# GpSimd adds the four feature blocks of the attention output's squares before TensorE sums over features

## The chip, the cores and the metric

The kernel runs on one core of a Trainium2 chip. The metric is the device time of one execution in microseconds (us). TensorE is called PE in the profile (PEld is its weight load), VectorE DVE, ScalarE ACT, GpSimd POOL and SyncE, which issues the loads and stores, SP.

## What is computed

One layer of a diffusion backbone for 128 context tokens and 512 latent tokens, with 1024 features, all in float32. Attention (8 query heads, 2 key heads of 64 features) and a gated short convolution run side by side, each gives 512 features, each is normalised over these, and one output projection joins them. A feed-forward part follows. The piece that matters:

```python
def _rms(x, g):
    y = x * lax.rsqrt(jnp.mean(x * x, axis=-1, keepdims=True) + RMS_EPS)
    return y * g

def _mixer(h, ...):
    proj = h @ w_in                       # q, k, v and the conv's gb, gc, u
    ...
    attn = _block_attention(q_r, k_all, v_all)       # (tokens, 512)
    y_conv = gb * _short_conv(gc * u, conv_w)        # (tokens, 512)
    merged = jnp.concatenate([_rms(attn, attn_out_norm), _rms(y_conv, conv_out_norm)], axis=-1)
    return merged @ w_out, k, v
```

The change touches the sum of `attn * attn` over the 512 features of a token, which is the first half of `_rms(attn, attn_out_norm)`.

## The kernel before, in words

The 640 tokens are five tiles of 128: tiles 0 to 3 are latent, tile 4 (`CTX`) is the context. Every product of two float32 matrices is made of three matmuls on rounded halves (`mm3`, L155 to L157; the convolution's own are L710 to L712). Each tile that such a matmul reads is made by `split`: ACT writes the rounded half (L151), DVE the rest (L152).

The span has four stages. Up to about 60 us inputs are loaded, normalised and modulated. From there to about 258 us attention and convolution run interleaved. The order of PE's instructions there is written out in the string `SEQ`: `S` are the scores of one head, `T` the transposes of its probabilities, `O` their product with the values, `Q` a transpose of queries, `F1` one step of the convolution as filler, and `r` the call of `att_rms`. From 258 to about 320 us the output projection runs, token tile by token tile in two halves of columns, and then the feed-forward part, to the end.

PE follows the program's order everywhere. In attention and projection DVE, ACT, POOL and SP follow an order that a scheduler set when the kernel was built, from its own costs and from the priorities in the code (`early`). Each engine takes its instructions strictly in that order, so an instruction that waits holds back all behind it on its engine.

The softmax of one head (`att_s`): PE writes the scores into `ps` (L824); DVE takes the maximum (L830); ACT scales it (L831) and takes the exponential (L834); DVE takes the reciprocal of the sum (L836); DVE (L840, first head of a pair) or ACT (L838, second head) scales the probabilities. The next scores wait until L834 has read `ps`, of which there is one buffer. `att_t` transposes the probabilities on PE (L851) and splits them, and `att_o` multiplies them with the values (L868).

When a pair of key and value heads of one tile is done, ACT copies its result out of PSUM (L875, for the context L934), SP moves halves of it across partitions by two DMAs into `es` (L883, L884), DVE adds (L889, L890), and `of[t]` holds 256 of the tile's 512 features: features on partitions, in four blocks of 128, tokens along the free dimension. ACT squares these into `osq[t]` (L891). For tile 3 `osq[t]` lies in the buffer `oz`. `v` is 0 for the first 256 features and 1 for the second.

`att_rms(t)` sums the squares over the features: the block of squares is PE's stationary operand, a column of ones the moving one, and the four blocks are added in PSUM. DVE then scales the sum (L163, `ms`), and POOL takes the power -1/2 (L165, `rA`). It is called for the context tile long after its attention, for tiles 0, 1 and 2 one or two units after theirs, and for tile 3 inside the output projection. There `conv_rms` has made the like factors `rB` for the convolution's half (L796 on PE, L163, L165), and each projected tile is scaled with `rA` (L1117 on ACT) and `rB` (L1118 on DVE), multiplied by a gate (L1120) and added to the input (L1121). L1029 are multiply-adds on DVE for a later gate, and L248 is DVE's half of the split of the output projection's weights.

Of the kernel before, what the change touches and what calls it, by code (L numbers as in the profile page):

```python
# [12 lines left out]
ALU = mybir.AluOpType  # L13
# [78 lines left out]
def build(ctx, tc, x_prompt, x_sample, c, cache_k, cache_v, c_ctx, norm_mix, norm_ffn, w_ada, b_ada,  # L92
# [3 lines left out]
    act, dve, pool, pe, sp = nc.scalar, nc.vector, nc.gpsimd, nc.tensor, nc.sync  # L96
# [23 lines left out]
    def T(tag, shape, dt=F32, bufs=1):  # L120
        seq[0] += 1
        return pools[where.get(tag, "A")][1].tile(list(shape), dt, tag=tag, bufs=bufs, name=f"{tag}_{seq[0]}")

    def PB(shape=(P, 512), dt=F32, tag="t"):
        seq[0] += 1
        if kept.get(tag):
            w = kept[tag].pop()
            n = 1
            for y in shape[1:]:
                n *= y  # L130
            w = w[:, :n] if tag != "s" else w
            if tag != "s" and len(shape) > 2:
                names = "abc"[:len(shape) - 1]
                w = w.rearrange("p (" + " ".join(names) + ") -> p " + " ".join(names), **dict(zip(names, shape[1:])))
            return w
        return pools["psum"][1].tile(list(shape), dt, tag=tag, bufs=pbufs[tag], name=f"p{tag}_{seq[0]}")
# [13 lines left out]
    def split(hi, lo, src):  # L150
        act.activation(hi, src, AF.Copy)  # L151
        dve.tensor_tensor(lo, src, f32(hi), ALU.subtract)  # L152
# [6 lines left out]
    def rstd_of(ss, n, scale, by=1.0, tag="rs"):  # L159

        w = ss.shape[1]
        ms = T("ms", (P, w), F32, 4)
        dve.tensor_scalar(ms, ss, scale * by, EPS * by, ALU.mult, ALU.add)  # L163
        r = T(tag, (P, w), F32, {"rB": 1, "rs": 6}.get(tag, NT))
        pool.tensor_tensor(r, ms, neghalf[:, :w], ALU.pow)  # L165
        return r
# [202 lines left out]
    ones = T("ones", (P, P))  # L369
# [445 lines left out]
    oe, osq = {}, {}  # L815
# [42 lines left out]
    def att_o(u, g):  # L858
        t, v, p = u[0:3]
        kts = GRPS[g]  # L860
        if g == 0:
            u[5] = PB((P, 2, P), tag="o")
        ov = u[5].rearrange("p a q -> p (a q)")
        last = g == len(GRPS) - 1
        for i, kt in enumerate(kts):
            w = VS[:, kt + 1, v].rearrange("p a d -> p (a d)")
            for n, x in enumerate(u[4][g]):
                pe.matmul(ov, w, x[:, i].rearrange("p a q -> p (a q)"), start=(g == 0 and i == 0 and n == 0),  # L868
                          stop=(last and i == len(kts) - 1 and n == 1))
        if not last:  # L870
            return
        if p == 0:
            oe[t, v] = T2((P, 2, 2, P))
        e = oe[t, v]
        act.activation(e[:, p], u[5], AF.Copy)  # L875
        if p == 0:
            return
        att_add(t, v, e)

    def att_add(t, v, e):  # L880

        esw = T("es", (P, 2, P))
        sp.dma_start(esw[0:64], e[64:128, :, 0, :])  # L883
        sp.dma_start(esw[64:128], e[0:64, :, 1, :])  # L884
        if v == 0:
            of[t] = T("of", (P, 4, P), F32, NT)
            osq[t] = T("osq", (P, 4, P), F32, OSQ) if t != NL - 1 else T("oz", (P, 4, P))
        o = of[t][:, 2 * v:2 * v + 2]
        dve.tensor_tensor(o[0:64], e[0:64, :, 0, :], esw[0:64], ALU.add)  # L889
        dve.tensor_tensor(o[64:128], e[64:128, :, 1, :], esw[64:128], ALU.add)  # L890
        act.activation(osq[t][:, 2 * v:2 * v + 2], o, AF.Square)  # L891
        if t == CTX:
            split(mix_ctx[0][:, 2 * v:2 * v + 2], mix_ctx[1][:, 2 * v:2 * v + 2], o)

# [33 lines left out]
    def ctx_o(v):  # L928
        ov = PB((P, 2, 2, P), tag="o")
        w = VS[:, 0, v].rearrange("p a d -> p (a d)")  # L930
        for n, x in enumerate(cu[v]):
            pe.matmul(ov.rearrange("p a b q -> p (a b q)"), w, x.rearrange("p h q -> p (h q)"), start=(n == 0), stop=(n == 1))
        e = T2((P, 2, 2, P))
        act.activation(e, ov, AF.Copy)  # L934
        att_add(CTX, v, e)

    def att_rms(t):
        sps = PB((P, 1))
        for p in range(4):
            pe.matmul(sps, osq[t][:, p], ones[:, 0:1], start=(p == 0), stop=(p == 3))  # L940
        rA[t] = rstd_of(sps, 1, 1.0 / 512, tag="rA")

    def unit(t, v, p):
# [10 lines left out]
    def rms_of(t):  # L954
        if t == CTX or t >= 0:
            att_rms(t)
# [121 lines left out]
    for j in range(2):  # L1078
        cols = slice(j * 512, (j + 1) * 512)
        for n, t in enumerate(TORD):  # L1080
# [23 lines left out]
            if j == 0 and n == 1:  # L1104
                att_rms(NL - 1)
                act.activation(warm, rA[NL - 1], AF.Silu)
# [25 lines left out]
            with early(XP[j]):  # L1132
# [3 lines left out]
                else:  # L1136
                    q = T("ms", (P, 1), F32, 4)
# [223 lines left out]
```

## Time and profile before

| what | value |
|---|---|
| runs, median (lowest to highest) of 3 | 758.66 us (757.63 to 758.73) |
| profiled execution: span from first to last instruction | 755.2 us |
| PE busy | 737.5 us, 98% |
| DVE busy | 551.7 us, 73% |
| ACT busy | 378.8 us, 50% |
| POOL busy | 42.6 us, 6% |
| chain that ended last: PE, DVE, ACT | 83%, 7%, 5% |

The page tells the profiled execution's span and no other time for it. The median of the timed runs lies 3.5 us above the span (758.66 - 755.2), for what lies ahead of the first and behind the last instruction. A PE that is busy for 98% says that it rarely stands idle in sight of the profile; matmuls overlap their neighbours, and a wait of under 0.15 us is not shown as one.

A row of the timeline has the start and the duration in us, the engine, the line, the operation, what it writes and reads, and how often it follows itself; in brackets stand the engine's idle time before it and what ended that. A row of the chain has start, duration and what.

### The profile page before, as it was taken

The numbers are of one execution on the slowest core, as the hardware profiler recorded it, in microseconds if no ns is written. First come the engines' busy times: TensorE is split into PE (matmuls) and PEld (weight loads), VectorE is DVE, ScalarE is ACT, GpSimd is POOL, SyncE is SP. The second block draws the span as 40 slices with busy tenths as digits, with TensorE's granted clock in tenths as the row PEclk, the third lists the DMA queues.
The fourth block names the chain that finished last, engine by engine and source line by source line (L and its number), as shares of the span: only waits on it lengthen the run. The fifth ranks groups of instructions, "written<-read, shape, count | busy, mean of one in ns | idle before, by whom it ended". The sixth has DMA issues, their size and how long they took to land.

```text
span 755.2 us, 11953 instructions
## 1 busy us (share of the span) xinstructions
PE 737.5 (98%) x4618; PEld 665.2 (88%) x4618; DVE 551.7 (73%) x997; ACT 378.8 (50%) x745; POOL 42.6 (6%) x75
## 2 busy tenths in 40 slices
PE   7999899999999999999999999999999999999997
PEld 5678888988998887899998799998889998899986
DVE  5558877666666798779979778884678866788653
ACT  5356777667656534765552235553125541255410
POOL 2403101011000110100000000000000000000000
PEclk9999999999999999999999999999999999999999
DMA  9985133532432464031235313133113232222312
GB/s 290 294 236 163 51 104 102 165 92 91 159 107 91 133 224 138 1 112 54 81 118 157 108 58 110 58 111 112 56 56 104 67 112 78 62 86 84 112 56 83
DMA packets 101389, 84.52 MB, mean 112 GB/s; under 512 B 3502, under 2 KB 81650, under 8 KB 101332
## 3 DMA queue, kind: packets, MB, share of 16 engines
q1 hardware_dynamic: 100980, 83.39, 35.9%
q8 instruction: 36, 0.59, 0.3%
q0 software_dynamic: 352, 0.37, 0.3%
q14 instruction: 21, 0.17, 0.1%
HBM read 79.68 MB, written 2.75 MB: 109 GB/s over the span
## 4 chain that ended last, share of the span: by engine, by line
PE 83%; DVE 7%; ACT 5%; DMA 2%; issue 1%; SPq 1%; POOL 0%; ACTq 0%
PE pf L155 17%; PE pf L157 17%; PE pf L156 17%; PE pc L710 3%; PE pc L712 3%; PE pc L711 3%; PE po L868 3%; PE ps L824 2%; PE ph L155 2%; PE ph L157 2%; PE ph L156 2%; PE pc L388 2%; PE pt L851 2%; DMA wf<-in_w_in_dram 1%; PE ps L155 1%
## 5 line engine op out<-in xcount | busy, mean ns | idle before, releaser
L151 ACT ACTIVATE wh<-wf 128x512 fp32r<-128x512 f32 (+1 forms) x68 | 55.5, 816 | 81.1 <-PE pf L157 59.3
L155 PE MATMUL pf<-wh,gT 128*128 128x512 f32 (+1 forms) x225 | 86.9, 386 | 0.0
L156 PE MATMUL pf<-wl,gT 128*128 128x512 f32 (+1 forms) x225 | 86.5, 385 | 0.0
L157 PE MATMUL pf<-wh,gT 128*128 128x512 f32 (+1 forms) x225 | 86.5, 384 | 0.0
L710 PE MATMUL pc<-hH,wh 128*128 128x320 f32 x192 | 61.1, 318 | 0.0
L712 PE MATMUL pc<-hH,wl 128*128 128x320 f32 x192 | 59.3, 309 | 0.0
L711 PE MATMUL pc<-hL,wh 128*128 128x320 f32 x192 | 59.3, 309 | 0.0
L152 DVE TENSOR_TENSOR wl<-wf,wh 128x1024 fp32r<-128x1024 f32 (+1 forms) x34 | 39.4, 1160 | 25.2 <-ACT wh L151 22.1
L155 PE MATMUL pf<-T,wh 128*128 128x320 f32 x160 | 49.6, 310 | 0.5 <-ACT u L1191 0.5
L156 PEld LDWEIGHTS pf<-wl,gT 128*128 128x128 f32 x225 | 42.3, 188 | 8.6 <-issue 0.2
L155 PEld LDWEIGHTS pf<-wh,gT 128*128 128x128 f32 x225 | 42.3, 188 | 8.6 <-issue 0.2
L157 PEld LDWEIGHTS pf<-wh,gT 128*128 128x128 f32 x225 | 42.3, 188 | 8.3
L156 PE MATMUL pf<-T,wh 128*128 128x320 f32 x160 | 49.4, 309 | 0.0
L155 PE MATMUL pf<-T,wl 128*128 128x320 f32 x160 | 49.4, 309 | 0.0
L156 PE MATMUL pf<-T,wl 128*128 128x320 f32 x160 | 49.4, 309 | 0.0
L157 PE MATMUL pf<-T,wl 128*128 128x320 f32 x160 | 49.4, 309 | 0.0
L157 PE MATMUL pf<-T,wh 128*128 128x320 f32 x160 | 49.4, 309 | 0.0
L155 PE MATMUL pf<-B,wl 128*128 128x320 f32 x152 | 47.1, 310 | 0.0
L157 PE MATMUL pf<-B,wl 128*128 128x320 f32 x152 | 47.0, 309 | 0.0
L156 PE MATMUL pf<-B,wl 128*128 128x320 f32 x152 | 47.0, 309 | 0.0
L155 PE MATMUL pf<-B,wh 128*128 128x320 f32 x136 | 42.2, 310 | 1.5 <-DVE cu L1220 1.5
L151 ACT ACTIVATE wl<-wf 128x512 fp32r<-128x512 f32 x34 | 21.2, 625 | 41.6 <-PE pf L156 34.8
(306 smaller groups left out, 2058.7 us busy)
## 6 DMA issues: line engine op xcount, KB each, us to landing
wf<-in_w_gate_up_dram SPq DMA_DIRECT2D x44, 512.0 KB, 4.0
aw<-in_w_ada_dram SPq DMA_DIRECT2D x24, 512.0 KB, 4.1
wf<-in_w_down_dram SPq DMA_DIRECT2D x20, 512.0 KB, 3.3
wf<-in_w_in_dram SPq DMA_DIRECT2D x18, 512.0 KB, 5.5
af<-in_w_ada_dram SPq DMA_DIRECT2D x32, 256.0 KB, 6.4
x<-in_x_sample_dram SPq DMA_DIRECT2D x8, 512.0 KB, 6.2
wf<-in_w_out_dram SPq DMA_DIRECT2D x8, 512.0 KB, 4.4
wf<-in_w_ada_dram SPq DMA_DIRECT2D x8, 512.0 KB, 3.7
```

Source lines behind the costliest of these rows:

```text
L151: act.activation(hi, src, AF.Copy)
L152: dve.tensor_tensor(lo, src, f32(hi), ALU.subtract)
L155: pe.matmul(out, lh, rh, start=start, stop=False, skip_group_check=more)
L156: pe.matmul(out, lh, rl, start=False, stop=False, skip_group_check=more)
L157: pe.matmul(out, ll, rh, start=False, stop=stop, skip_group_check=more)
L388: pe.matmul(out[CG * g:CG * (g + 1)], cp[:, k], w, start=(k < 4), stop=(k >= KD - 4), skip_group_check=True)
L710: pe.matmul(acc, wh[:, k], hH[k][:, c0:c0 + n], start=(k == 0), stop=False)
L711: pe.matmul(acc, wh[:, k], hL[k][:, c0:c0 + n], start=False, stop=False)
L712: pe.matmul(acc, wl[:, k], hH[k][:, c0:c0 + n], start=False, stop=(k == KD - 1))
L824: pe.matmul(s2[:, g, :320], q, kk[:, v, P + g * 320:P + (g + 1) * 320], start=(i == 0), stop=(i == 1))
L851: pe.transpose(tp[:, i, h], u[3][h][:, kt * P:(kt + 1) * P], ident)
L868: pe.matmul(ov, w, x[:, i].rearrange("p a q -> p (a q)"), start=(g == 0 and i == 0 and n == 0), stop=(last and i == len(kts) - 1 and n == 1))
```

## The change

When the second half of a tile's squares has been written (`v` is 1), POOL adds features 256 to 511 to features 0 to 255, and then the second of the two remaining blocks to the first, in place. One matmul per tile then sums the 128 partitions of the first block, in place of four.

```diff
         act.activation(osq[t][:, 2 * v:2 * v + 2], o, AF.Square)
+        if v:
+            q = osq[t]
+            pool.tensor_tensor(q[:, 0:2], q[:, 0:2], q[:, 2:4], ALU.add)
+            pool.tensor_tensor(q[:, 0], q[:, 0], q[:, 1], ALU.add)
...
     def att_rms(t):
         sps = PB((P, 1))
-        for p in range(4):
-            pe.matmul(sps, osq[t][:, p], ones[:, 0:1], start=(p == 0), stop=(p == 3))
+        pe.matmul(sps, osq[t][:, 0], ones[:, 0:1], start=True, stop=True)
         rA[t] = rstd_of(sps, 1, 1.0 / 512, tag="rA")
```

The line numbers behind L891 grow by three or four: the adds are L894 and L895, the matmul of `att_rms` is L943 where it was L940. PE and ACT keep their order, but for the 15 matmuls that go.

POOL's order, first piece: the context tile. `c` is the convolution's padded buffer, `rq` the factor of a tile's queries. Before:

```order
L165 TENSOR_TENSOR rs_1078<-ms_1076,neghalf_176 128x2
L165 TENSOR_TENSOR rq_1237<-ms_1235,neghalf_176 128x8
L729 MEMSET c_291_1263 128x1 x4
L165 TENSOR_TENSOR rA_1514<-ms_1512,neghalf_176 128x1
L165 TENSOR_TENSOR rq_1573<-ms_1571,neghalf_176 128x8
```

Now:

```order
L165 TENSOR_TENSOR rs_1078<-ms_1076,neghalf_176 128x2
L165 TENSOR_TENSOR rq_1239<-ms_1237,neghalf_176 128x8
L729 MEMSET c_291_1265 128x1 x4
L894 TENSOR_TENSOR osq_1112<-osq_1112 128x256
L895 TENSOR_TENSOR osq_1112<-osq_1112 128x128
L165 TENSOR_TENSOR rA_1513<-ms_1511,neghalf_176 128x1
L165 TENSOR_TENSOR rq_1572<-ms_1570,neghalf_176 128x8
```

The two adds stand where POOL had nothing to do until `rA`.

POOL's order, second piece: tiles 2 and 3, up to the factors of the output projection. Before:

```order
L751 TENSOR_TENSOR ysum_727<-ysum_727,c_601_2718 128x512
L751 TENSOR_TENSOR ysum_727<-ysum_727,c_601_2718 128x128
L729 MEMSET c_654_2942 128x1 x4
L165 TENSOR_TENSOR rA_2855<-ms_2853,neghalf_176 128x1
L751 TENSOR_TENSOR ysum_727<-ysum_727,c_707_3221 128x512
L751 TENSOR_TENSOR ysum_727<-ysum_727,c_707_3221 128x128
L165 TENSOR_TENSOR rB_3315<-ms_3313,neghalf_176 128x5
L165 TENSOR_TENSOR rA_3397<-ms_3395,neghalf_176 128x1
```

Now:

```order
L751 TENSOR_TENSOR ysum_727<-ysum_727,c_601_2715 128x512
L751 TENSOR_TENSOR ysum_727<-ysum_727,c_601_2715 128x128
L894 TENSOR_TENSOR osq_2514<-osq_2514 128x256
L895 TENSOR_TENSOR osq_2514<-osq_2514 128x128
L729 MEMSET c_654_2938 128x1 x4
L165 TENSOR_TENSOR rA_2851<-ms_2849,neghalf_176 128x1
L751 TENSOR_TENSOR ysum_727<-ysum_727,c_707_3217 128x512
L751 TENSOR_TENSOR ysum_727<-ysum_727,c_707_3217 128x128
L894 TENSOR_TENSOR oz_3007<-oz_3007 128x256
L895 TENSOR_TENSOR oz_3007<-oz_3007 128x128
L165 TENSOR_TENSOR rB_3313<-ms_3311,neghalf_176 128x5
L165 TENSOR_TENSOR rA_3392<-ms_3390,neghalf_176 128x1
```

Tile 2's adds stand ahead of the convolution's memsets, and tile 3's adds ahead of `rB`.

DVE's order at tile 2's `att_rms`; `nsr` holds a head's softmax scalars, `ms` the scaled sum of squares. Before:

```order
L889 TENSOR_TENSOR of_2516<-t_583_2624,es_2759 64x256
L890 TENSOR_TENSOR of_2516<-t_583_2624,es_2759 64x256
L152 TENSOR_TENSOR pl_2812<-pt_2808,ph_2811 128x256
L830 TENSOR_REDUCE nsr_2820<-ps_2815 128x1
L836 RECIPROCAL nsr_2820<-nsr_2820 128x1
L163 TENSOR_SCALAR ms_2853<-pt_2848 128x1
L830 TENSOR_REDUCE nsr_2866<-ps_2861 128x1
```

Now:

```order
L889 TENSOR_TENSOR of_2513<-t_583_2621,es_2756 64x256
L890 TENSOR_TENSOR of_2513<-t_583_2621,es_2756 64x256
L152 TENSOR_TENSOR pl_2811<-pt_2807,ph_2810 128x256
L830 TENSOR_REDUCE nsr_2819<-ps_2814 128x1
L163 TENSOR_SCALAR ms_2849<-pt_2847 128x1
L836 RECIPROCAL nsr_2819<-nsr_2819 128x1
L830 TENSOR_REDUCE nsr_2862<-ps_2857 128x1
```

`ms`, which waits for the matmul on the squares, now stands ahead of the softmax's reciprocal.

## The prediction

> **What bounds the kernel now.** I read the page first, then the chain that ended last for the five matmul groups that change, then the stages around them.
>
> ```profile
> span 755.2 us, 11953 instructions
> ...
> PE 737.5 (98%) x4618; PEld 665.2 (88%) x4618; DVE 551.7 (73%) x997; ACT 378.8 (50%) x745; POOL 42.6 (6%) x75
> ...
> PE 83%; DVE 7%; ACT 5%; DMA 2%; issue 1%; SPq 1%; POOL 0%; ACTq 0%
> ```
>
> PE carries the span and POOL is nearly empty, so taking work from PE to POOL can pay. The chain shows where the removed matmuls lie (start, duration, what):
>
> ```profile
> 116.65 0.79 PE pt L940 x8
> 155.13 1.05 PE pt L940 x8
> 195.40 0.79 PE pt L940 x8
> 226.18 0.79 PE pt L940 x8
> 270.93 0.79 PE pt L940 x8
> ```
>
> In this order they are the context tile and tiles 0, 1, 2, 3. All five lie on the chain. Four matmuls show as eight passes, each of which loads 128 columns of squares to multiply them with a single column. But PE is not equally the bound everywhere. Three stretches (length, then PE, PEld, DVE, ACT, POOL busy):
>
> ```profile
> 90.00:120.00 30.00, 28.11 (x199) 24.52 (x198) 23.02 (x44) 21.55 (x46) 1.13 (x1) 1.00 0.37 115
> 180.00:210.00 30.00, 30.00 (x225) 27.81 (x225) 19.38 (x39) 20.58 (x44) 0.56 (x1) 1.00 0.35 115
> 262.00:292.00 30.00, 30.00 (x147) 25.21 (x146) 28.21 (x48) 14.08 (x27) 3.27 (x2) 1.00 0.61 208
> ```
>
> From 180 to 210 PE never stands. At 90 to 120 it waits for 1.89 us: the softmax paces it. From 262 to 292 DVE has 28.21 of 30 us, as good as full, and whatever delays DVE there comes back to PE.
>
> **What goes.** Of eight passes two stay. Six of eight in 0.79 us are 0.59 us a tile (tile 2: 226.02 to the next instruction's start is about the same), 2.96 us for five. I take 0.59 for tile 0 as well, whose 1.05 holds a wait for a PSUM buffer.
>
> What of it is kept depends on what is late next. For the context tile, tile 0 and tile 1 I found no wait behind the matmul that began ahead of it and ends within 0.6 us of its need, so each keeps 0.59: 1.77. Tile 2 is different:
>
> ```profile
> 224.01 0.42 ACT L891 ACTIVATE osq<-of 128x256 f32<-128x256 f32 x1 [0.66 <-DVE of L890]
> 224.35 0.81 DVE L830 TENSOR_REDUCE nsr<-ps 128x1 f32<-128x640 f32 x1
> ...
> 226.02 0.95 PE L940 MATMUL pt<-ones,osq 128*128 128x1 f32 x8
> ...
> 226.71 0.16 DVE L836 RECIPROCAL nsr<-nsr 128x1 f32<-128x1 f32 x1 [1.55 <-ACT pr L834]
> ...
> 226.91 0.83 ACT L838 ACTIVATE pr<-pr,nsr 128x640 f32<-128x640 f32 x1 [0.23 <-DVE nsr L836]
> 227.00 0.16 DVE L163 TENSOR_SCALAR ms<-pt 128x1 f32<-128x1 f32 x1
> ...
> 227.25 0.55 POOL L165 TENSOR_TENSOR rA<-ms,neghalf 128x1 f32<-128x1 f32 x1 [8.96 <-DVE ms L163]
> ...
> 227.74 1.04 PE L851 MATMUL pt<-ident,pr 128*128 128x128 f32 x8
> ```
>
> The transposes at 227.74 need the second head's probabilities, which ACT finishes at 226.91 + 0.83 = 227.74, on a softmax chain (L830, L836, L838) that began ahead of the matmul. PE would be there 0.59 us sooner and wait. Only the first transpose, one of eight in 1.04, needs nothing of L838: 0.13 kept. For tile 3:
>
> ```profile
> 292.08 0.74 DVE L248 SCALAR_TENSOR_TENSOR wl<-wf,vec,wh 128x512 fp32r<-128x512 f32 x1
> ...
> 293.08 0.40 PE L156 MATMUL ph<-wl,mx 128*128 128x512 f32 x1
> ```
>
> PE takes the weights' lower half at 293.08, and the full DVE queue made it at 292.82. Of tile 3's 0.59 only these 0.26 are kept. Kept in all: 1.77 + 0.13 + 0.26 = 2.16 us.
>
> **What is added.** Two adds on POOL per tile. Their sizes have near rows:
>
> ```profile
> L564 POOL TENSOR_TENSOR tab<-oz,gnk 128x256 f32<-128x256 f32 x1 | 0.7, 727 | 0.0
> ```
>
> ```profile
> L751 POOL TENSOR_TENSOR ysum<-ysum,c x6: 465/970/1815, 174.0 to 260.8; 128x512 f32<-128x512 f32 x3, 128x128 f32<-128x128 f32 x3
> ```
>
> 128x256 is 0.73 us, 128x128 at its shortest 0.47: 1.20 us a tile. The hand-over from DVE to POOL was 0.09 us (L163 ends at 227.16, rA starts at 227.25). So the matmul can start some 1.3 us behind the end of the squares. The squares end for the second half, in the order of tiles 0, 1:
>
> ```profile
> 144.94 0.42 ACT L891 ACTIVATE osq<-of 128x256 f32<-128x256 f32 x1
> ```
>
> ```profile
> 186.64 0.42 ACT L891 ACTIVATE osq<-of 128x256 f32<-128x256 f32 x1 [1.12 <-DVE of L890]
> ```
>
> Against the matmuls at 155.13 and 195.40 that leaves over 8 us of cover. The context tile has from 94.85 (its row is below) to 116.65. Tile 2 has 226.02 - 224.43 = 1.59 us, so the adds just fit, with 0.3 to spare; and a stall of up to 0.59 would cost nothing, since L838 is waited for anyway. DVE's new order, `ms` ahead of L836, costs nothing either unless the matmul is late: two passes from 226.02 end about 226.4, `ms` is done ahead of 226.71.
>
> The cost that the durations do not show is that POOL and DVE hinder each other. The rows of before:
>
> ```profile
> 259.21 2.25 POOL L751 TENSOR_TENSOR ysum<-ysum,c 128x512 f32<-128x512 f32 x2 [31.42 <-ACT c L749]
> ```
>
> ```profile
> L1027 DVE TENSOR_SCALAR aacc<-wf,cs x2: 689/1108/1528, 259.6 to 261.1; 128x512 f32<-128x512 f32 x2
> L1027 DVE TENSOR_SCALAR cg<-wf,cs x2: 477/482/486, 397.3 to 404.1; 128x512 f32<-128x512 f32 x2
> ```
>
> ```profile
> 275.01 1.58 POOL L165 TENSOR_TENSOR rA<-ms,neghalf 128x1 f32<-128x1 f32 x1 [5.38 <-DVE ms L163]
> ```
>
> The same DVE instruction takes 0.48 us alone and 1.53 beside POOL's add at 259.21: DVE stood 1.05 us for POOL. And the same power takes POOL 0.55 us at 227.25 but 1.58 at 275.01, beside a busy DVE. [...]
>
> Two tiles have such DVE work on the path beside their adds. The context tile:
>
> ```profile
> 94.45 0.40 ACT L891 ACTIVATE osq<-of 128x256 f32<-128x256 f32 x1
> ...
> 94.60 0.56 PE L824 MATMUL ps<-KA,qT 128*128 128x320 f32 x2 [0.95 <-ACT pr L834]
> ...
> 94.78 0.55 DVE L840 TENSOR_SCALAR pr<-pr,nsr 128x640 f32<-128x640 f32 x1
> ...
> 95.25 0.42 DVE L152 TENSOR_TENSOR m<-of,m 128x256 fp32r<-128x256 f32 x1
> ...
> 95.58 0.82 DVE L830 TENSOR_REDUCE nsr<-ps 128x1 f32<-128x640 f32 x1
> ```
>
> Squares end at 94.85, the first add is ready at about 94.95, while L840 runs; at 95.33 either the add or L152 goes. If the add goes, L152 and behind it the maximum L830 come 0.73 us later, and the scores' exponential and the next scores on PE with them, since here PE waits for the softmax (0.95 us at 94.60). Bounds: 0 and 0.73. I take 0.5, nearer the upper end, because at 259.21 POOL, which had waited through a DVE instruction, went first.
>
> Tile 3:
>
> ```profile
> 266.29 0.42 ACT L891 ACTIVATE oz<-of 128x256 f32<-128x256 f32 x1 [3.62 <-DVE of L890]
> ...
> 267.90 0.69 DVE L152 TENSOR_TENSOR mx<-of,mx 128x512 fp32r<-128x512 f32 x1
> 267.94 1.69 POOL L165 TENSOR_TENSOR rB<-ms,neghalf 128x5 f32<-128x5 f32 x1 [6.47 <-DVE ms L163]
> ...
> 269.67 0.75 DVE L1118 SCALAR_TENSOR_TENSOR mix<-ph,rB,mix 128x512 f32<-128x512 f32 x1 [1.08 <-POOL rB L165]
> ```
>
> The adds now stand ahead of `rB` on POOL, and DVE's L1118 waits for `rB` with all of the full stretch behind it. Unhindered they run from 266.8 to 268.0, and `rB` is 0.06 us late. At worst they wait until L152 ends at 268.59, and `rB` starts at 268.59 + 1.20 = 269.79, which is 1.85 late. I take 0.5: POOL gets in behind one of the two L1029 that run from 266.29. Tiles 0, 1 and 2 I cost at nothing: 8 us of cover, or a maximum from PSUM on DVE.
>
> **The sum.** 2.16 - 0.5 - 0.5 = 1.2 us off the span of 755.2; the median lies 3.5 us above that span, and the same taken from it gives 758.66 - 1.2 = 757.5 us. The two unknown costs at their lower ends (0 and 0.06) give 756.6, at their upper ends (0.73 and 1.85) 759.1.
>
> **Rivals.** A: all that is removed is kept. The softmax chain behind tile 2 and DVE's queue behind tile 3 move along, POOL finds gaps. For it: PE at 30.00 of 30 from 180 to 210. Against it: the two rows with 227.74 and 292.82. Between 2.2 and 2.96 us, so 755.7 to 756.4.
>
> B, slower: DVE starves the adds as it does the powers, by 1.58 / 0.55 = 2.9 times, so a pair takes 3.45 us. Then tile 2's matmul starts at 224.53 + 3.45 = 227.98, 1.96 late, of which 0.59 is free: 1.37; and `rB` starts at 270.25, 2.31 late, less the 0.26 at L248: 2.05. Against the 1.77 of the other three tiles that is 1.65 us slower, 760.3. It decides from a pair of 2.63 us on, where 1.77 = (2.63 - 2.08) + (2.63 - 1.40). Against it: larger adds on POOL were stretched by only 1.4 (L751, 1815 ns), and beside tile 2's adds DVE mostly reduces from PSUM.
>
> C: the softmax paces PE in all of attention, and the 1.77 is not kept. Then 0.39 is left, less the two costs of 1.0: 759.3. For it: the waits at 90 to 120. Against it: the stretch at 180 to 210.
>
> **Chances.** A measurement of this kernel can tell about 0.2% (1.5 us) from no change. Forecast 0.58: it passes 1.5 us where the two costs stay under 0.64 together, which I give 0.26 of the 0.58; 0.32 is within. A 0.20, faster. C 0.08, within. B 0.14, slower. So faster 0.46, same 0.40, slower 0.14. The range holds the forecast's 756.6 to 759.1 and reaches into A and C: 755.9 to 759.2; the forecast's own is 756.6 to 759.1.
>
> **What would show it.** Right: L943 in two passes of about 0.2 us; at tile 2 PE idle ahead of L851 with ACT named; L152 behind the context's squares or L1118's wait for `rB` longer by some tenths. Wrong: a wait for POOL ahead of L943 at tile 2 (B), no new wait at all (A), PE idle grown by 0.6 behind each of the first three matmuls (C), or adds far from 0.73 and 0.47.

## The result, and the profile after

| | median (lowest to highest), runs | ratio to before, 95% interval |
|---|---|---|
| before, beside the changed kernel | 758.51 us (757.63 to 759.36), 6 | |
| after | 755.82 us (755.57 to 756.58), 6 | 0.9968 [0.9959, 0.9978] |

The change takes 2.7 us off by the medians, 0.3% (2.4 us) by the ratio; 1.2 were forecast. The profiled execution of the changed kernel took 755.83 us with a span of 754.1, so 1.7 us lie around its span. The page of after, its span, engines, the queue of instruction packets and the chain:

```profile
span 754.1 us, 11909 instructions
PE 735.8 (98%) x4588; PEld 662.6 (88%) x4588; DVE 552.2 (73%) x997; ACT 378.5 (50%) x745; POOL 49.4 (7%) x85
q8 instruction: 36, 0.59, 0.3%
PE 78%; DVE 10%; ACT 5%; DMA 3%; issue 2%; POOL 1%; SPq 0%; ACTq 0%; DVEq 0%
```

PE lost 30 passes and 1.7 us of work, POOL won ten adds and 6.8 us. The span fell by 1.1 us only (755.2 to 754.1), the time by 2.7; the difference is the subject of the experiments. The adds at the context tile, tile 2 and tile 3, from the timeline of POOL in after:

```profile
94.67 0.99 POOL L894 TENSOR_TENSOR osq<-osq 128x256 f32<-128x256 f32 x1 [4.97 <-ACT osq L891]
95.74 0.52 POOL L895 TENSOR_TENSOR osq<-osq 128x128 f32<-128x128 f32 x1
223.14 0.74 POOL L894 TENSOR_TENSOR osq<-osq 128x256 f32<-128x256 f32 x1 [6.97 <-ACT osq L891]
223.96 0.46 POOL L895 TENSOR_TENSOR osq<-osq 128x128 f32<-128x128 f32 x1
265.42 0.85 POOL L894 TENSOR_TENSOR oz<-oz 128x256 f32<-128x256 f32 x1 [5.33 <-ACT oz L891]
266.35 0.80 POOL L895 TENSOR_TENSOR oz<-oz 128x128 f32<-128x128 f32 x1
267.11 1.70 POOL L165 TENSOR_TENSOR rB<-ms,neghalf 128x5 f32<-128x5 f32 x1
```

At tile 2 a pair takes 0.74 + 0.46 us, as costed. What DVE did beside the other two pairs, from its timeline in after:

```profile
94.52 0.55 DVE L840 TENSOR_SCALAR pr<-pr,nsr 128x640 f32<-128x640 f32 x1
94.98 0.96 DVE L152 TENSOR_TENSOR m<-of,m 128x256 fp32r<-128x256 f32 x1
95.87 0.81 DVE L830 TENSOR_REDUCE nsr<-ps 128x1 f32<-128x640 f32 x1
...
264.92 1.90 DVE L1032 SCALAR_TENSOR_TENSOR aacc<-wf,cs,aacc 128x512 f32<-128x512 f32 x2
...
266.82 0.15 DVE L163 TENSOR_SCALAR ms<-pt 128x5 f32<-128x5 f32 x1
...
268.85 0.75 DVE L1121 SCALAR_TENSOR_TENSOR mix<-ph,rB,mix 128x512 f32<-128x512 f32 x1 [1.08 <-POOL rB L165]
```

L152 took 0.42 us before and takes 0.96 beside the add; the two multiply-adds (L1029 of before) took this together:

```profile
266.29 1.42 DVE L1029 SCALAR_TENSOR_TENSOR aacc<-wf,cs,aacc 128x512 f32<-128x512 f32 x2
```

1.42 became 1.90. Both lines read two tensors from SBUF. The adds beside them took longer too: the first 0.99 us at the context tile and 0.85 at tile 3, for 0.74 at tile 2, and the second 0.80 at tile 3 for 0.46. The maximum L830, which reads PSUM, takes 0.81 beside the second add at the context tile and 0.81 beside the first at tile 2, and 0.81 to 0.83 in all its 32 places, in before and in after. On PE, the matmul at tile 2, the next scores, and the last rows of the projection:

```profile
224.47 0.38 PE L943 MATMUL pt<-ones,osq 128*128 128x1 f32 x2 [0.19 <-POOL osq L895]
225.37 0.56 PE L824 MATMUL ps<-KA,qT 128*128 128x320 f32 x2 [0.17 <-ACT pr L834]
...
226.06 1.35 PE L851 MATMUL pt<-ident,pr 128*128 128x128 f32 x8
...
291.52 0.50 PE L156 MATMUL ph<-wl,mx 128*128 128x512 f32 x1 [0.30 <-DVE wl L248]
```

Two passes in 0.38 us in place of eight in 0.95. The eight passes of transposes at 226.06 take 1.35 us and not 1.04, since the second of them, which starts at 226.43, waits for L838 and holds back the rest. ACT's row in after shows L838 (it ends at 226.38):

```profile
225.55 0.83 ACT L838 ACTIVATE pr<-pr,nsr 128x640 f32<-128x640 f32 x1 [0.23 <-DVE nsr L836]
```

At L156 PE now waits 0.30 us for DVE's L248, where it waited for nothing before.

Setting the start of each PE instruction in after against the same one in the first profile of before gives where the 1.1 us come from: the context's adds cost 0.53 and give 0.16 back; the matmuls give 0.67, 0.61 and 0.66 (context, tiles 0 and 1); tile 2 gives 0.21 and loses 0.74; tile 3 gives 0.67 and loses 0.57 at L248. Together that is 1.14. PE is also 0.24 ahead by 90, where nothing has changed yet, and loses 0.34 from 293 to the end; two executions of the unchanged kernel differ by 0.1 to 0.2 at such places too.

### The profile page after: what moved, and what is told of

Read it like the earlier page. It is cut to its first block, busy times and chain, and to the rows that moved or that the text cites. A ratio compares the mean times of both kernels' runs of the same rounds, so it can differ in the third digit from the quotient of the medians.

```text
span 754.1 us, 11909 instructions
## 1 busy us (share of the span) xinstructions
PE 735.8 (98%) x4588; PEld 662.6 (88%) x4588; DVE 552.2 (73%) x997; ACT 378.5 (50%) x745; POOL 49.4 (7%) x85
## 4 chain that ended last, share of the span: by engine, by line
PE 78%; DVE 10%; ACT 5%; DMA 3%; issue 2%; POOL 1%; SPq 0%; ACTq 0%; DVEq 0%
PE pf L155 17%; PE pf L156 17%; PE pf L157 17%; PE pc L710 3%; PE pc L711 3%; PE pc L712 3%; PE ps L824 2%; PE pc L388 2%; PE po L868 2%; PE pt L851 2%; PE ps L155 1%; PE ph L156 1%; PE ph L157 1%; DMA af<-in_w_ada_dram 1%; PE ph L155 1%
## 5 line engine op out<-in xcount | busy, mean ns | idle before, releaser
L156 PE MATMUL pf<-wl,gT 128*128 128x512 f32 (+1 forms) x225 | 86.5, 385 | 0.0
L152 DVE TENSOR_TENSOR wl<-wf,wh 128x1024 fp32r<-128x1024 f32 (+1 forms) x34 | 39.4, 1160 | 25.2 <-ACT wh L151 22.3
L156 PEld LDWEIGHTS pf<-wl,gT 128*128 128x128 f32 x225 | 42.3, 188 | 8.5 <-issue 0.2
L156 PE MATMUL pf<-T,wl 128*128 128x320 f32 x160 | 49.4, 309 | 0.0
L156 PE MATMUL pf<-T,wh 128*128 128x320 f32 x160 | 49.4, 309 | 0.0
L156 PE MATMUL pf<-B,wl 128*128 128x320 f32 x152 | 47.0, 309 | 0.0
L1273 DVE TENSOR_TENSOR dm<-pf,g 128x512 f32<-128x512 f32 (+1 forms) x41 | 27.7, 675 | 20.1 <-PE pf L157 20.1
```

Of the source, the lines that this page charges most:

```text
L156: pe.matmul(out, lh, rl, start=False, stop=False, skip_group_check=more)
L1273: dve.tensor_tensor(dm, ps[:, :n], g2[cc][:, oc], ALU.mult)
```

## Experiments

Two theories to begin with. Theory 1: the sum stands, a like pair of executions differs by 1.1 to 1.2 us, the adds cost about 1.0 of what the matmuls give, and the first profile of before was a quick execution. Theory 2: the timed runs tell, the change gives 2.4 us and the adds cost nothing. The changes here are against the kernel before, if not said otherwise.

**The two kernels again, side by side.** Both unchanged.

> The kernel before, unchanged, timed against itself. The trace of after ends 1.13 us ahead of that of before (754.1 against 755.2), but the timed runs differ by 0.32% (2.4 us). Theory 1 (the two traces tell what the change does, and the profiled execution of before was a quick one of its kind): ratio 1.000 within 0.001, a span of 756 to 757.5 in the new profile, and the difference from the first profile lies at places that the change does not touch. Theory 2 (the first profile of before is typical, and the change gains 2.4 us): the span comes back at 755.2 within 0.3.

> The changed kernel, unchanged, on the same chip as the other three. Theory 1: 1.1 to 1.5 us below before (ratio 0.998 to 0.9985). Theory 2: 2.4 us below (0.9968).

Before: 758.04 us (757.54 to 760.26, 11 runs), ratio to its like 1.0005 [0.9996, 1.0014], profiled 757.88 with a span of 756.1. After: 756.24 (755.69 to 757.54, 9 runs), ratio 0.9975 [0.9966, 0.9985], profiled 755.69 with a span of 753.9. So 1.7 to 1.8 us lie around the span in all these runs, and the first profile of before, with 755.2, was an execution of about 757.0, quick by 1.7 against the 758.66 of its three timed runs and by 1.0 against the 758.04 here. The new one is 0.92 us longer at its end; PE falls back by 0.53 at 207 and 0.63 at 228, both behind moves of halves across partitions (`es`) that DVE waits for. DVE in the first profile of before:

```profile
186.19 0.42 DVE L890 TENSOR_TENSOR of<-t,es 64x256 f32<-64x256 f32 x1 [1.53 <-DMA es<-t]
202.37 0.42 DVE L889 TENSOR_TENSOR of<-t,es 64x256 f32<-64x256 f32 x1
223.10 0.42 DVE L889 TENSOR_TENSOR of<-t,es 64x256 f32<-64x256 f32 x1 [0.48 <-DMA es<-t]
```

In before again:

```profile
186.17 0.42 DVE L890 TENSOR_TENSOR of<-t,es 64x256 f32<-64x256 f32 x1 [1.65 <-DMA es<-t]
202.76 0.42 DVE L889 TENSOR_TENSOR of<-t,es 64x256 f32<-64x256 f32 x1 [0.55 <-DMA es<-t]
224.16 0.42 DVE L889 TENSOR_TENSOR of<-t,es 64x256 f32<-64x256 f32 x1 [1.12 <-DMA es<-t]
```

And in after:

```profile
183.52 0.42 DVE L890 TENSOR_TENSOR of<-t,es 64x256 f32<-64x256 f32 x1
200.43 0.41 DVE L889 TENSOR_TENSOR of<-t,es 64x256 f32<-64x256 f32 x1
221.74 0.42 DVE L889 TENSOR_TENSOR of<-t,es 64x256 f32<-64x256 f32 x1 [1.01 <-DMA es<-t]
```

These are the moves of tile 1's second half of features (its second move for short), and of tile 2's first and second. Each move is two DMAs of 64 KB: L883 brings what L889 adds, L884 what L890 adds. The first two waits are gone with the change, though it touches no move. Against before again, after again ends 2.21 us earlier; beside the terms above, PE is 0.60 earlier from 207 on, where it had waited for the product that tile 2's first move delays, and loses 0.11 at tile 2 in place of 0.74. A like pair thus differs by 2.2 us by the spans and by 1.8 by the medians: more than the 1.1 to 1.2 of theory 1, less than the 2.4 of theory 2.

**One matmul without the adds, and the adds with four matmuls.** First the matmul alone, which leaves three of the four blocks out of the sum, then the adds alone, which count three blocks more than once.

```diff
-        for p in range(4):
-            pe.matmul(sps, osq[t][:, p], ones[:, 0:1], start=(p == 0), stop=(p == 3))
+        pe.matmul(sps, osq[t][:, 0], ones[:, 0:1], start=True, stop=True)
```

> The removal alone: one matmul per tile on the first block of squares, no adds on GpSimd, so three of four feature blocks are left out of the sum of squares. VectorE's order has the scaled sum ahead of the reciprocal at tile 2, as in after. Theory 1 (the adds cost about 0.5 us at the context tile and 0.5 at tile 3): 2.2 to 2.6 us below before, ratio 0.997, and 1.0 below after; in the trace no shift of 0.5 us behind 95 us, and the 0.6 to 0.7 of tiles context, 0 and 1 in full. Theory 2 (the adds cost nothing): the same time as after.

754.95 us (754.88 to 756.75, 5 runs), ratio 0.9965 [0.9952, 0.9977], span 753.2: 0.7 us under after again by the spans, 1.3 by the medians. Both costs of the adds are gone there (0.54 us at 98, of which after again makes 0.15 good, and 0.6 at 291); 0.4 is lost at tile 2, whose second move is waited for 1.40 us and not 1.01.

```diff
+        if v:
+            q = osq[t]
+            pool.tensor_tensor(q[:, 0:2], q[:, 0:2], q[:, 2:4], ALU.add)
+            pool.tensor_tensor(q[:, 0], q[:, 0], q[:, 1], ALU.add)
```

> The adds alone: GpSimd adds as in after, but four matmuls per tile sum all four blocks as before, so that parts of the squares are counted twice. Theory 1: 1.0 us above before (0.5 at the context tile, where VectorE's split of m stands 0.5 us for the add, and 0.5 at tile 3 through rB), ratio 1.001, and no wait at tile 2, where the order of VectorE is that of before. Theory 2: no difference from before in time, and none in the trace behind 95 and 293 us.

758.31 us (757.65 to 759.46, 11 runs), ratio 0.9999 [0.999, 1.0008]: the rise by 1.0 us that theory 1 expects did not come. PE is late by 0.55 at 98, gets 0.16 of it back at 101, and is late by nothing at tile 3; the profiled execution ends 0.46 behind before again. So the adds cost about what theory 1 says in the changed kernel, at its two places, and the part of theory 2 by which they cost nothing falls. Without the adds tile 3 keeps its whole 0.67:

```profile
291.11 0.43 PE L156 MATMUL ph<-wl,mx 128*128 128x512 f32 x1
```

PE does not wait here (0.30 and 0.36 us in the two profiles of after). With four matmuls PE is not there early enough to notice DVE's delay. Both are needed for that cost.

**What holds up the moves.** The q8 row says 36 packets of 16 KB. PE has 4618 matmuls and as many weight loads, 9236 / 36 = 257 a packet: by this count they bring PE's instructions. Bytes moved in before again (40 slices of 0.04 us each; the columns of the queue rows are packets, MB, share of 16 engines), from 183.3 and from 184.2:

```profile
GB/s 39 13 0 410 0 0 38 77 128 192 192 205 192 179 167 90 64 13 0 0 0 0 0 0 0 0 0 0 0 0 0 0 0 0 0 0 0 0 0 0
...
q8 instruction: 1, 0.02, 5.8%
...
GB/s 0 0 0 0 0 0 0 0 0 0 0 0 0 0 0 0 0 13 0 13 13 13 0 13 13 0 13 13 0 0 0 0 0 0 0 0 0 0 0 0
```

The slice with 410 is a packet of 16 KB, booked at its start, 183.4. It takes 5.8% of 16 engines' 1.6 us, 1.5 us of one engine. The second DMA of tile 1's second move is done in the slices to 184.0, but for nine packets that trickle out one by one (13) to 185.3; L890 starts at 186.17. Nine is a sixteenth of the 144 packets of such a DMA (288 for a move's two, from 139.2 to 142.0 in after): one engine's part, if they are spread evenly. In after, from 183.3:

```profile
GB/s 0 0 0 0 0 0 0 0 0 0 0 0 0 0 0 0 0 0 0 0 0 0 0 0 0 410 0 0 0 0 0 0 0 0 0 0 0 0 0 0
```

The packet comes at 184.3, when the move is over. The traces also hold sixteen completions of each DMA, as many as there are engines. Of this one, fifteen came by 184.34 in before again and the last at 186.14; in after all came by 183.31. Over all runs, a packet starts 0.2 to 1.6 us behind the issue of twenty of these DMAs. In each of the twenty the fifteenth completion comes 2.0 to 2.1 us behind the issue, as without a packet, and the sixteenth 1.1 to 1.4 us behind the packet's end. Twelve PE instructions fewer a tile (six passes, six loads) put the packets later in the program, while the program runs earlier. That is theory 3; theory 4 is that the moves are quick because they start earlier against the loads. To tell them apart, PE instructions were added that do nothing else: matmuls of one element.

```diff
+    for _ in range(9):          # 13 in the kernel before
+        pe.matmul(cps[0:1, 0:1], ones[0:1, 0:1], ones[0:1, 0:1], start=True, stop=True)
     pe.transpose(cps, crow, ident[:16, :16])
```

> The changed kernel, with nine matmuls of one element by one element ahead of PE's first work, where PE stands idle until 3.02 us; each shows as two passes with a weight load each, so 36 PE instructions more, and nothing else moves. Theory 3: PE's instructions come in packets of 16 KB on one of the DMA engines (spaced some 16.7 us, the time in which PE runs about 250 instructions); in the kernel before two of these packets (183.4 and 200.3) fall into the moves of halves across partitions for tiles 1 and 2 and hold them up, and with the change, by fewer PE instructions, they miss them (184.3 and 200.8). 36 instructions more bring them 36 / 15 = 2.4 us earlier, to about 182 and 198.4, back into the moves: DVE waits again for tile 1's second move (L890, 1.5 us against none), tile 2's first is ready about 0.5 us later, PE is 0.5 us later from about 207 on, and the time rises by 0.4 to 0.8 us against the changed kernel (756.0), to some 756.6. Theory 4: the moves are quick in the changed kernel because they start earlier against the loads around them. Then nothing changes: L890 waits for nothing, 756.0.

757.53 us (756.71 to 759.04, 11 runs), ratio 0.9993 [0.9985, 1.0002]. The packets came at 183.8 and 199.5, L890 waited 1.45 us again, and tile 2's first move took 2.96 us from issue to landing (2.04 in after again), as theory 3 says. Its price was missed: nothing was lost at 207, 0.57 us at 226 (the second move was waited for 1.60 us and not 1.01), and 1.3 by 35: the packet that came at 23.3 in after again came at 17.5 here, among the first loads, and PE waited 1.5 us for `af` (0.5 in after again). That the packet is the cause there was not tested by itself.

> The kernel before, with thirteen matmuls of one element ahead of PE's first work: 52 PE instructions more, and nothing else moves. Theory 3: the instruction packets come 3.5 us earlier, from 183.4 and 200.5 to about 179.9 and 197.0, ahead of the moves that start at 181.7 and 199.1: DVE's wait of 1.5 us for tile 1's second move goes, and so does the one of 0 to 0.55 us for tile 2's first; PE is up to 0.55 us earlier from 207 on, and the time falls by 0.3 to 0.6 us, from 758.0 to about 757.5. Theory 4: the waits stay, 758.0.

758.25 us (757.14 to 758.85, 11 runs), ratio 0.9999 [0.999, 1.0008]. All three waits shrank, to 0.30, 0 and 0.15 us (tile 1's first addition, L889 of before, waited 0.82 in place of 0.38), and PE made good 1.2 us between 200 and 230 against before again; 2.1 us had been lost by 35, again at `af`. The time alone would have spoken for theory 4; the waits speak for theory 3. So the instructions were put where they do not touch the start, into the wait of PE for the softmax at 94:

```diff
-S0.0 F1 F1 S0.1
+S0.0 F1 F1 P13 S0.1        # P15 in the changed kernel; P<n>: n matmuls of one element
```

> The kernel before with thirteen matmuls of one element in the same wait (0.95 us): 52 PE instructions more. Theory 3: packets from 183.4, 200.5 and 217.3 to about 179.9, 197.0 and 213.8; DVE's waits for the moves (1.5 to 1.65 for tile 1's second, 0 to 0.55 for tile 2's first, 0.5 to 1.1 for tile 2's second) shrink below 0.4, 0.1 and 0.3; PE is 0.6 to 1.1 us earlier by 230, and the time falls to 757.0 to 757.6 from 758.1. Theory 4: 758.1.

756.93 us (756.63 to 758.09, 11 runs), ratio 0.9989 [0.998, 0.9998]. Packets at 182.0, 197.5 and 213.6; DVE's rows for the three moves:

```profile
184.16 0.42 DVE L889 TENSOR_TENSOR of<-t,es 64x256 f32<-64x256 f32 x1 [0.71 <-DMA es<-t]
...
184.75 0.42 DVE L890 TENSOR_TENSOR of<-t,es 64x256 f32<-64x256 f32 x1
202.24 0.41 DVE L889 TENSOR_TENSOR of<-t,es 64x256 f32<-64x256 f32 x1
222.64 0.42 DVE L889 TENSOR_TENSOR of<-t,es 64x256 f32<-64x256 f32 x1
```

The three that waited don't wait any more. The packet at 182.0 still falls on the first DMA of tile 1's second move, so its L889 waits 0.71 us (0.38 in before again), which costs PE nothing. PE ends 1.17 us earlier than in before again: 0.61 at 207 and 0.63 at 228. The kernel before gets quicker by 26 passes that compute nothing, by 1.1 us by the medians and 0.8 by the ratio. Theory 3 stands.

> The changed kernel with fifteen matmuls of one element ahead of the scores for which PE waits 0.93 us at 94.3 (30 passes of 0.03 us, so the wait covers them): 60 PE instructions more, and nothing at the start of the kernel moves. Theory 3: the packets of PE's instructions come 60 / 15 = 4.0 us earlier behind that place: from 184.4, 200.9 and 219.4 to about 180.4, 196.9 and 215.4, ahead of all three moves (180.6, 197.4 and 216.5). DVE's wait of 1.01 us for tile 2's second move shrinks to 0.1 to 0.5, PE is 0.3 to 0.7 us earlier behind 226, and the time is 755.5 to 755.9 against the changed kernel's 756.1. Theory 4: nothing changes, 756.1; if the small matmuls cost their 0.97 us, 757.1.

756.23 us (755.44 to 756.71, 8 runs), ratio 0.9978 [0.9968, 0.9988], a miss: no gain. The packets moved by 2.5 to 3.6 us and not 4.0; the first, at 182.0, fell on tile 1's second move (L889 waited 0.90 us), and the third came at 215.8, with the loads issued at 215.88 ahead of tile 2's second move, whose wait stayed at 1.02.

**Which tiles pay.** The change for some tiles alone.

```diff
+        if v and t in (0, 1):          # (0, 1, CTX) in the second
...
+        n = 1 if t in (0, 1) else 4
```

> Adds and one matmul for tiles 0 and 1 alone; the context, tile 2 and tile 3 keep their four matmuls. By theory 1 these two tiles give 0.6 to 0.67 us each with nothing given back: 1.2 to 1.35 us, 756.7, and up to 0.5 more where tile 2's move is met by no instruction packet (theory 3: 24 PE instructions fewer ahead of it, as many as in the changed kernel; 12 fewer ahead of tile 1's), so 756.2 to 756.7. DVE's L152 of the context takes 0.42 us again and not 0.96, PE waits for no DVE at L248 of the projection beyond what it did. By theory 2 (the adds cost nothing) it loses three tiles' 0.59 us against the changed kernel, and would be 1.2 to 1.8 us slower than that: 757.5 to 758.

757.36 us (756.93 to 758.53, 11 runs), ratio 0.999 [0.9981, 0.9999], slower than expected by 0.7. PE is 1.57 us ahead of before again at 227, as theories 1 and 3 say, and 0.7 less ahead of 229: tile 2's second move, with a packet at 219.6 among the loads ahead of it, is waited for 1.80 us. (In its profiled execution the granted clock was also 0.58 from 228 to 232, so its end can't be compared.)

> Adds and one matmul for the context and tiles 0 and 1; tiles 2 and 3 keep four matmuls. Theory 1: against the kernel of tiles 0 and 1 alone the context tile gives 0.67 us at its matmul and gives 0.5 us back at its adds (DVE's L152 0.96 us again): 0.1 to 0.3 us quicker, 756.0 to 756.5; against the changed kernel as quick, since tile 2 keeps only 0.1 to 0.2 us there and tile 3 gives back 0.6 of its 0.67. Theory 2: 0.6 us quicker than the kernel of tiles 0 and 1, and 0.6 to 1.2 us slower than the changed one.

756.44 us (755.7 to 757.77, 10 runs), ratio 0.9976 [0.9967, 0.9985]. By the profile the context tile gives 0.3 net (0.55 lost at its adds, 0.16 and 0.67 gained), as expected; the other 0.6 against the kernel of tiles 0 and 1 fits tile 2's second move, waited for 1.01 here and 1.80 there. Tiles 2 and 3 of the changed kernel add 0.3 (2.21 against 1.88 us ahead of before again), within the spread of the times.

**Better than both?** In the changed kernel the context's second squares, and with them its adds, go behind two other instructions of ACT:

```diff
-        act.activation(osq[t][:, 2 * v:2 * v + 2], o, AF.Square)
...
+        if t != CTX or not v:
+            squares(t, v)       # the square and, for v = 1, the adds
...
-O0.0 F1 O0.1 O0.2 S2.0
+O0.0 F1 O0.1 O0.2 z4 S2.0        # z4: squares(CTX, 1)
```

> The changed kernel with the context tile's second squares two instructions later in ACT's order (behind L151 and L724), so that its adds meet the maximum L830, which reads PSUM, and not L152. Theory 1: L152 takes 0.42 us and not 0.96, the scores behind it come 0.5 us earlier (PE at 97.7), and 0.3 to 0.5 us of that lasts to the end: 755.6 to 755.8 against 756.1. Rival: the adds only meet another instruction of DVE (L152 of the weights, 1.2 us long, behind the maximum), which is held instead; then 756.1 or more.

755.64 us (755.24 to 757.69, 11 runs), ratio 0.9972 [0.9964, 0.9981]. DVE's rows at the context tile:

```profile
95.44 0.42 DVE L152 TENSOR_TENSOR m<-of,m 128x256 fp32r<-128x256 f32 x1
95.78 0.82 DVE L830 TENSOR_REDUCE nsr<-ps 128x1 f32<-128x640 f32 x1
96.66 1.46 DVE L152 TENSOR_TENSOR wl<-wf,wh 128x1024 fp32r<-128x1024 f32 x1
```

The first add ran beside the maximum and cost nothing; the second met the weights' L152 (1.46 us for 1.21). PE gained 0.55 us at 98 and lost 0.37 at 101.6, so both expectations hold in part. By the median it is the quickest that computes all; its interval overlaps that of after again. The last run added 22 matmuls of one element in two waits of PE:

```diff
-S0.0 F1 F1 S0.1 ... S1.0 F1 T0.0 S1.1
+S0.0 F1 F1 P11 S0.1 ... S1.0 F1 T0.0 P11 S1.1
```

> The changed kernel with the context's squares later (as in the run before) and 22 matmuls of one element, eleven in each of two waits of PE for the softmax (0.91 and 0.96 us; 22 passes of 0.032 us are 0.70 us each): 88 PE instructions more. Sixty moved the packets by 3.3 to 3.6 us, so these move them by about 5: from 184.7, 201.2 and 219.6 to about 179.7, 196.2 and 214.6, ahead of all three moves, and of the loads (issued at 215.3) that tile 2's second move stands behind. Theory 3: DVE's wait for that move, 1.0 us in the changed kernel, and still so where the packet fell on the start of these loads (215.8), falls below 0.3; PE is 0.3 to 0.7 us earlier behind 226; 754.9 to 755.4 against 755.6. Rival: that wait is of the loads alone, stays at 1.0, and the time is 755.6, or 756 if the small matmuls aren't covered.

757.17 us (756.09 to 758.5, 11 runs), ratio 0.999 [0.9978, 1.0001], where 754.9 to 755.4 were expected. Tile 2's second move was not waited for any more, and PE made good 0.85 us there. But an earlier packet, at 149.5 in the run before, now came at 140.9, into tile 0's second move. Bytes from 140.8, and DVE and PE behind it, in this run:

```profile
GB/s 128 154 205 627 218 179 167 90 64 39 13 0 0 0 0 51 102 166 192 179 192 205 179 129 77 52 13 0 0 0 0 0 0 0 0 0 0 0 0 0
...
143.66 0.42 DVE L897 TENSOR_TENSOR of<-t,es 64x256 f32<-64x256 f32 x1 [3.44 <-DMA es<-t]
...
146.33 0.56 PE L824 MATMUL ps<-KA,qT 128*128 128x320 f32 x2 [1.41 <-ACT pr L834]
```

DVE's wait was 1.48 us in the run before; PE lost 2.0 us. One packet on one move is worth that much.

## Why the prediction was right and wrong

- **What goes** (0.59 us a tile): 0.61 to 0.67 by PE's starts. Right, a little low. That the context and tiles 0 and 1 keep theirs: 1.94 for 1.77, right.
- **Tile 2** (0.13 kept, L838 next): L838 ends at 226.4 in after and the transposes wait for it; 0.10 kept in the second pair. `ms` ahead of the reciprocal cost nothing, as said. The 0.74 lost in the first pair is more than this step allowed: it holds the longer wait for the second move (1.01 for 0.48).
- **Context adds** (0.5): 0.53, less 0.16 made good. Place and size right: L152 took 0.54 us longer beside the add. That L152 would stand for the whole of the first add (0.73), the upper bound, was an estimate; no run shows it.
- **Tile 3** (0.26 kept, 0.5 lost, through `rB`): 0.67 given, 0.57 lost, so 0.10 gained for 0.24 lost. Amount of the loss right, place wrong: behind `ms` (it ends at 266.97) `rB` starts 0.14 us later, 0.08 in before, so the adds ahead of it on POOL cost it 0.06. The loss is on DVE: L1032 takes 0.48 us longer, and behind it stand `ms`, which `rB` needs, and DVE's queue up to L248. The wait of L1121 (L1118 of before) for `rB` stayed at 1.08. That 0.26 bounds what is kept was wrong: without the adds DVE's queue moves along and all is kept.
- **The sum** (1.2): 1.1 between the two profiles that it spoke of.
- **The time** (757.5; measured 755.82 and 756.24): here it failed, at "the median lies 3.5 us above that span". 1.7 to 1.8 lie around a span, so this execution was some 1.7 quicker than the median; 0.9 of that, what sets it off from before again, lies behind the moves. The rest is mostly the median of three runs itself: 758.66, and 757.99 to 758.33 in four later series of 14 to 32 runs of the kernel before. The forecast took a quick execution's waits for the typical ones.
- **The step that was missing**: no term asked whether the change would touch the waits for the moves, though one of 1.53 us stood in the trace. That one went and gave PE nothing; but tile 2's first move, waited for 0.02 us in the profile read and 0.32 to 0.55 in two others with four matmuls, went with it, and gave 0.6 us at 207 against before again.
- **The range and the rivals**: the first measurement lies 0.08 us below the range, the second inside it. Rival A's figure (755.7 to 756.4) holds it, but A's reason doesn't: L838 and L248 were waited for. **B** fell: pairs of 1.20 to 1.65 us, far from 2.63. **C** fell: the three matmuls kept 1.94.

Of the 0.9 us between the two profiles of the unchanged kernel, the part at 207 is a packet's: it started 1.06 us behind the issue of tile 2's first move in the one and 1.58 in the other, and the move landed 3.14 and 3.67 us behind its issue. What stays open: why the packet came later there, and how the 0.63 at tile 2's second move divides between its packet (217.0 and 217.3), the loads and its later issue.

## What to carry to other kernels

Before a forecast takes a profile as typical, compare its execution's own time with the median; where only the span is known, take what lies around it as unknown, not as the difference. An edit that changes how many instructions a busy engine has can also shift the packets that bring them (sixty more moved them by 2.5 to 3.6 us here): look for small transfers that someone waits for and that are issued shortly ahead of such a packet (0.2 to 1.6 us here). An add on POOL was cheap in cover (tiles 0 and 1 kept 0.61 and 0.66 us), and cost where it met a DVE instruction with two operands from SBUF on the path (0.54 and 0.48 us here); the maximum from PSUM was a good neighbour for it (0.81 us beside it, and 0.81 to 0.83 elsewhere).

## What the runs showed that was not expected

A packet of PE's instructions takes 0.9 to 1.5 us of one DMA engine mostly, and comes every 15 to 22 us in attention here. A 64 KB DMA has to wait for that engine: the last of its sixteen completions came 1.1 to 1.4 us behind the end of a packet that met it. From issue to landing it took 2.0 to 2.1 us in six of the ten moves of after, where no packet started in the 1.6 us behind the issue, and 2.4 to 4.1 with one. A packet held 257 instructions by the count above, and for the transfers beside them the packets had a price: 0.6 us at 207, 2.0 us at 146 in the last run, and probably the 1.3 to 2.1 us among the first loads.
